# MLP of a hybrid attention block: weights loaded half a pair ahead, the up product's accumulators outside the down product's ring, rectification on ScalarE

## The chip, the cores and the metric

The kernel runs on one core of a Trainium2 chip. A core has a tensor engine (PE; its weight loads are listed as PEld), a vector engine (VectorE, DVE), a scalar engine (ScalarE, ACT), GpSimd (POOL) and a sync engine (SP) whose queue issues the DMA transfers here. Every engine takes its own instructions in the order of the program and waits on semaphores for the others. The metric is the device time of one execution in microseconds; lower is better.

## The reference

One transformer block on 1024 tokens of width 1024: a norm, an input projection, two kinds of attention (a mixture of dilated windows, and a compressed, selected and windowed one), an output projection with a residual, and an MLP with a squared rectifier. The change is in the MLP alone:

```python
h = rms_norm(h_res, norm_mlp[l])                       # 1024 tokens x 1024
h_res = h_res + jnp.square(jax.nn.relu(h @ w_up[l])) @ w_down[l]   # hidden width 4096
return rms_norm(h_res, norm_final)
```

## The kernel before, in words

The attention part fills about the first 700 us of the execution; then the MLP runs to the end. All matrices are float32. A product keeps float32's accuracy by splitting each operand into a rounded part and a residual (`hi` and `lo`) and adding three matmuls: hi with hi, lo with hi, hi with lo. `split` (line 92) makes the two parts: a copy on ScalarE writes `hi` (line 94), a subtraction on VectorE writes `lo` (line 95).

**Pairs.** The hidden width is cut into 16 pairs of 256 columns, `g` = 0 to 15. A pair has two blocks of 128 columns, f = 0 and 1. The tokens are cut into two halves of 512, h = 0 and 1.

**First matrix (up).** The pair's product is two column blocks by two token halves, with the inner width 1024 in two halves as well: a two by two block product. It is done with seven block products in place of eight, y1 to y7 (`prod`, line 1059), each 4 x 3 = 12 matmuls of 128x512 into one PSUM bank, 84 a pair. The weight combinations for them are made by `w_prep` and `w_split` from four raw blocks: RW[g, 0] to RW[g, 3], in buffers `cA`, `r3`, `r2` and `cB`; the split weights lie in `wa` to `we` (`wa` serves y1 and y5, `wb` y4 and y3, `wc` y6, `wd` y2, `we` y7). The token combinations (B11, B21, B22, T1 to T4) are made once, at the start of the MLP. The four results, of shape 128 columns x 512 tokens, are

```
c11 = y1 + y2                c12 = y1 + y6 + y5 + y3
c21 = (y1 + y6 + y7) - y4    c22 = (y1 + y6 + y7) + y5
```

so c12 and c22 are sums that live in a buffer from the first term to the last. c11 and c21 are of the first token half, c22 and c12 of the second.

**Rectification.** `c_done` (line 1069) squares the rectified result in place on VectorE (line 1071: max with 0, times itself), copies it to `uh` on ScalarE (1072), and subtracts on GpSimd for the residual `ul` (1073). The four pairs of `uh` and `ul` lie in v0, v1 (c11), v2, v3 (c21), u0, u1 (c12) and u2, u3 (c22).

**Second matrix (down).** `down` (line 1113) takes the eight tiles of 128 tokens in turn, the first half's four first. For each tile and each of two halves of 512 output columns one bank collects 2 x 3 = 6 matmuls (lines 1124 to 1126; `dn` is the split w_down of the pair, one tile for each f), and VectorE adds the bank, times the norm's factor of each token, to the residual stream `st` (line 1127). 16 banks, 96 matmuls a pair. The raw w_down blocks are loaded by `d_load` into u2 and u3, two blocks for each, and split by `d_split`. The last pair's `down` adds the final norm and the stores.

**Buffers and banks.** Each named buffer exists once, so a new tile of a name waits for the last reader of the old one. PSUM has eight banks of 128x512: rings T (2), O (2), F (1) and S (3). Before the change, y1 and y6 take T, y4 and y7 O, y2 F, and y5 and y3 take S, which is also the ring of `down`.

**What sets the order.** A scheduler orders every engine's instructions when the program is built, by the priority of the program's own order and by its estimates of when inputs and buffers are ready; the order is then fixed. It mixes the pairs: part of the up product of pair g + 1 runs between the down products of pair g.

## Time and profile before

| | us |
|---|---|
| median of 3 runs (lowest, highest) | 1413.13 (1410.70, 1417.88) |
| profiled execution, its own time | 1414.72 |
| span of that execution, first to last instruction | 1412.9 |
| mean granted tensor clock, share of full speed | 0.98 |
| PE, PEld busy | 1313.4, 1110.6 |
| DVE, ACT, POOL busy | 970.4, 650.3, 512.0 |

A row of a timeline gives the start in microseconds from the span's start, the duration, the engine, the line, the operation, output and inputs by the program's names without numbers, a count, and in brackets how long the engine had been idle before it and what it waited for. A row of a group ends with the busy time, the mean duration of one in ns, and the idle time ahead of the group by what ended it. In a row of windows each engine has its busy time and in parentheses its instructions; then come the granted clock, the DMA engines' busy share and GB/s. A few matmul records are missing from the trace, and matmuls overlap, so their starts tell more than their durations.

### The profile page before, as it was taken

Reading aid. Unit: us, or ns where it says so; the run is one execution under the profiler, and the core shown is the slowest. Engines: PE = TensorE matmul, PEld = TensorE weight load, DVE = VectorE, ACT = ScalarE, POOL = GpSimd, SP = SyncE. Lnnn points to the kernel's source line nnn. Section 1 sums busy time; section 2 is a strip of 40 time slices with the busy share of each in tenths; the row PEclk is TensorE's granted clock in tenths of the full one; section 3 lists DMA queues with packets and bytes.
Section 4 is the critical chain, followed back from the end, with each engine's and each line's share of the span. In section 5 each row is a group of like instructions: output and inputs, shape, how many; then the busy total and the mean of one; then the engine's idle time right before and its main releaser. Section 6 shows DMA issues by size and latency. Waiting matters only on the chain.

```text
span 1412.9 us, 23742 instructions
## 1 busy us (share of the span) xinstructions
PE 1313.4 (93%) x8891; PEld 1110.6 (79%) x8891; DVE 970.4 (69%) x1953; ACT 650.3 (46%) x1212; POOL 512.0 (36%) x724
## 2 busy tenths in 40 slices
PE   7999999998987999899778999999999999999996
PEld 6788989888976777677656888888888888788885
DVE  6664565773458876878587667677767667776767
ACT  7462755872557866898553222222222212222216
POOL 3445473664445665577542110011111001111115
PEclk9999999999898999999999999999999999999998
DMA  6265382985538986686311121112111111111113
GB/s 189 68 113 120 87 185 51 206 184 145 93 107 180 172 152 129 143 157 96 82 30 34 56 59 46 45 46 60 45 60 46 59 41 50 55 50 61 45 46 134
DMA packets 265747, 131.68 MB, mean 93 GB/s; under 512 B 220064, under 2 KB 240544, under 8 KB 265632
## 3 DMA queue, kind: packets, MB, share of 16 engines
q1 hardware_dynamic: 265488, 129.90, 40.0%
q8 instruction: 70, 1.15, 0.3%
q14 instruction: 45, 0.37, 0.1%
q10 hardware_dynamic: 144, 0.26, 0.0%
HBM read 68.26 MB, written 8.39 MB: 54 GB/s over the span
## 4 chain that ended last, share of the span: by engine, by line
PE 57%; DVE 16%; DMA 8%; issue 7%; POOL 6%; ACT 5%; SPq 1%; DVEq 0%; POOLq 0%; ACTq 0%
PE S L1124 8%; PE S L1125 7%; PE S L1126 7%; PE F L335 3%; PE F L336 3%; PE F L337 3%; DMA u<-in_w_down_dram 3%; PE O L1064 2%; PE O L1063 2%; PE T L1065 2%; PE T L1063 2%; PE T L1064 2%; PE O L1065 2%; PE S L418 2%; DVE c L1071 1%
## 5 line engine op out<-in xcount | busy, mean ns | idle before, releaser
L1073 POOL TENSOR_TENSOR ul<-c,uh 128x512 fp32r<-128x512 f32 x64 | 92.5, 1454 | 557.8 <-ACT uh L1072 555.9
L1127 DVE SCALAR_TENSOR_TENSOR st<-S,r,st 128x512 f32<-128x512 f32 (+1 forms) x257 | 185.8, 742 | 70.3 <-PE S L1126 69.7
L1124 PE MATMUL S<-dn,uh 128*128 128x512 f32 (+1 forms) x514 | 203.2, 396 | 9.6 <-DVE c L1110 5.9
L1126 PE MATMUL S<-dn,ul 128*128 128x512 f32 (+1 forms) x514 | 200.6, 391 | 0.8 <-POOL ul L1073 0.8
L1125 PE MATMUL S<-dn,uh 128*128 128x512 f32 (+1 forms) x514 | 200.8, 391 | 0.0
L335 PE MATMUL F<-wh,hh 128*128 128x256 f32 (+1 forms) x576 | 167.2, 292 | 6.1 <-DVE st L214 3.2
L336 PE MATMUL F<-wl,hh 128*128 128x256 f32 (+1 forms) x576 | 166.5, 289 | 2.3 <-DVE wl L95 2.3
L337 PE MATMUL F<-wh,hl 128*128 128x256 f32 (+1 forms) x576 | 165.4, 288 | 0.0
L1124 PEld LDWEIGHTS S<-dn,uh 128*128 128x128 f32 x514 | 97.2, 189 | 37.8 <-DVE c L1110 12.2
L434 ACT ACTIVATE ns<-ns,mn 128x640 f32<-128x640 f32 (+7 forms) x152 | 110.7, 747 | 35.1 <-POOL mn L433 21.7
L335 PEld LDWEIGHTS F<-wh,hh 128*128 128x128 f32 x576 | 110.7, 193 | 8.2 <-DVE st L214 3.6
L450 POOL TENSOR_TENSOR hl<-ns,hl 128x640 f16<-128x640 f32 (+5 forms) x67 | 105.5, 1575 | 30.9 <-ACT hl L448 24.9
L1126 PEld LDWEIGHTS S<-dn,ul 128*128 128x128 f32 x514 | 97.0, 189 | 22.0 <-POOL ul L1073 1.5
L336 PEld LDWEIGHTS F<-wl,hh 128*128 128x128 f32 x576 | 111.3, 193 | 3.7 <-DVE wl L95 3.1
L1125 PEld LDWEIGHTS S<-dn,uh 128*128 128x128 f32 x514 | 97.4, 190 | 19.2
L337 PEld LDWEIGHTS F<-wh,hl 128*128 128x128 f32 x576 | 111.0, 193 | 0.5
L448 ACT ACTIVATE hl<-ns 128x640 f16<-128x640 f32 (+5 forms) x115 | 91.2, 802 | 5.8 <-DMA pt<-hl 5.0
L468 PE MATMUL O<-v,pt 128*128 128x65 f16 x694 | 77.3, 195 | 15.9 <-DMA pt<-hl 13.4
L1081 ACT ACTIVATE c<-T 128x512 f32<-128x512 f32 x15 | 9.0, 599 | 172.2 <-PE S L1125 172.2
L468 PEld LDWEIGHTS <-pt 128*128 128x128 f16 x694 | 63.9, 99 | 27.6 <-DMA pt<-hl 17.4
L418 PE MATMUL S<-kb,qb 128*128 128x384 f32 (+3 forms) x192 | 72.9, 385 | 12.6 <-DVE mn L429 8.9
L433 POOL TENSOR_SCALAR mn<-mn 128x1 f32<-128x1 f32 x130 | 43.7, 336 | 96.4 <-DVE mn L429 81.2
(372 smaller groups left out, 3625.1 us busy)
## 6 DMA issues: line engine op xcount, KB each, us to landing
u<-in_w_down_dram SPq DMA_DIRECT2D x64, 256.0 KB, 2.8
wr<-in_w_in_dram SPq DMA_DIRECT2D x44, 256.0 KB, 2.9
r<-in_w_up_dram SPq DMA_DIRECT2D x32, 256.0 KB, 2.7
st<-in_x_dram SPq DMA_DIRECT2D x8, 512.0 KB, 5.9
wor<-in_w_out_dram SPq DMA_DIRECT2D x16, 256.0 KB, 3.5
cA<-in_w_up_dram SPq DMA_DIRECT2D x16, 256.0 KB, 2.8
cB<-in_w_up_dram SPq DMA_DIRECT2D x16, 256.0 KB, 2.6
ns<-in_xT_dram SPq DMA_DIRECT2D x7, 512.0 KB, 5.1
```

Source lines behind the costliest of these rows:

```text
L335: pe.matmul(ps, hh[:, k, ts], hi, start=k == 0, stop=False)
L336: pe.matmul(ps, hh[:, k, ts], lo, start=False, stop=False)
L337: pe.matmul(ps, hl[:, k, ts], hi, start=False, stop=k == KD - 1)
L418: pe.matmul(ps[:, :w], u["q"], u["k"][:, cs], start=True, stop=False)
L434: u["exp"] = act.activation(ns[:, :n * 128], ns[:, :n * 128], AF.Exp, scale=-1.0, bias=mn[:, j:j + 1])
L450: pool.tensor_sub(lo, p, hi)
L468: pe.matmul(ps, ph, v[:, 64:129], start=t == 0, stop=False)
L1073: pool.tensor_sub(lo, a, f32(hi))
L1124: pe.matmul(ps, uh[:, ts], wd[:, 0, cs], start=j == 0, stop=False)
L1125: pe.matmul(ps, uh[:, ts], wd[:, 1, cs], start=False, stop=False)
L1126: pe.matmul(ps, ul[:, ts], wd[:, 0, cs], start=False, stop=j == 1)
L1127: dve.scalar_tensor_tensor(o[:, cs], ps, r2[:, t:t + 1], o[:, cs], op0=OP.mult, op1=OP.add)
```

## The change

Five things change in the MLP, and the order of the engines follows from them.

1. `d_load`: from pair 1 on, the four w_down blocks have four buffers, v0 to v3 (those of the first token half's `uh` and `ul`), and are requested in the middle of the pair before, after its fifth down tile. All four splits stand at the head of `up`.
2. `w_load`: all four raw w_up blocks of the next pair are requested in the middle of `up`, where two of them were requested after it. For that, c12 has a buffer of its own, `x`, and c22 takes u0, after c11.
3. Banks: y2 and y7 move to T, y5 to O and y3 to F, so S is left to `down` alone.
4. `c_done`: ReLU and Square on ScalarE, both in place, then `split`: a copy on ScalarE and a subtraction on VectorE. GpSimd does none of it.
5. With the third, the second half's results (`f1`: c22, with y5 added to c12; `f2`: c12) are written into the program after the first and the second down tile (`c_rest`), where they stood at the end of `up`. The steps of `w_prep` keep their places.

```diff
     def d_load(g, q):
         j, c = q % 2, q // 2
-        t = RD[g, q] = small("u%d" % (2 + j))
+        t = RD[g, q] = small("v%d" % q if g else "u%d" % (2 + j))
...
     def c_done(g, f, h, a):
         hi, lo = U[g, f, h] = [small(x, F32R, "uh" if n == 0 else "ul") for n, x in enumerate(UT[f, h])]
-        dve.scalar_tensor_tensor(a, a, 0.0, a, op0=OP.max, op1=OP.mult)
-        act.activation(hi, a, AF.Copy)
-        pool.tensor_sub(lo, a, f32(hi))
+        act.activation(a, a, AF.Relu)
+        act.activation(a, a, AF.Square)
+        split(hi, lo, a)
 
     def up(g):
-        y = {n: bank(x, [128, 512], 2) for n, x in ((1, "T"), (4, "O"), (6, "T"), (2, "F"), (7, "O"), (5, "S"), (3, "S"))}
-        for q in range(2):
-            d_load(g, q)
+        y = {n: bank(x, [128, 512], 2) for n, x in ((1, "T"), (4, "O"), (6, "T"), (2, "T"), (7, "T"), (5, "O"), (3, "F"))}
+        for q in range(4):
+            d_split(g, q)
         prod(g, 1, y[1])
         c11 = small("u0", name="c11")
         act.activation(c11, y[1], AF.Copy)
         w_split(g, 5, "a", RW[g, 2])
-        for q in range(2):
-            d_split(g, q)
-        for q in range(2, 4):
-            d_load(g, q)
         prod(g, 4, y[4])
         prod(g, 6, y[6])
-        c12 = small("cA", name="c12")
+        c12 = small("x", name="c12")
         dve.tensor_add(c12, y[6], c11)
         w_split(g, 3, "b", RW[g, 1])
-        w_load(g + 1, 2, "r2")
-        w_load(g + 1, 1, "r3")
+        for blk, tag in enumerate(("cA", "r3", "r2", "cB")):
+            w_load(g + 1, blk, tag)
         prod(g, 2, y[2])
         dve.tensor_add(c11, y[2], c11)
         c_done(g, 0, 0, c11)
         prod(g, 7, y[7])
-        c22 = small("cB", name="c22")
+        c22 = small("u0", name="c22")
...
         c_done(g, 1, 0, c21)
-        for q in range(2, 4):
-            d_split(g, q)
         prod(g, 5, y[5])
-        dve.tensor_add(c22, y[5], c22)
-        dve.tensor_add(c12, y[5], c12)
-        c_done(g, 1, 1, c22)
         prod(g, 3, y[3])
-        dve.tensor_add(c12, y[3], c12)
-        c_done(g, 0, 1, c12)
+        return c_rest(g, y, c12, c22)
+
+    def c_rest(g, y, c12, c22):
+        def f1():
+            dve.tensor_add(c22, y[5], c22)
+            dve.tensor_add(c12, y[5], c12)
+            c_done(g, 1, 1, c22)
+
+        def f2():
+            dve.tensor_add(c12, y[3], c12)
+            c_done(g, 0, 1, c12)
+
+        return [f1, f2]
...
         else:
-            w_load(g + 1, 0, "cA")
-            w_load(g + 1, 3, "cB")
-        jobs = [] if last else w_prep(g + 1)
+            late += w_prep(g + 1)
         for i, t in enumerate(TO):
             down(g, t, last)
-            if i >= 2 and jobs:
-                jobs.pop(0)()
+            if late:
+                late.pop(0)()
+            if i == 4 and not last:
+                for q in range(4):
+                    d_load(g + 1, q)
```

The code ahead of the loop, which does pair 0, is changed in the same way.

**VectorE at the end of a middle pair's up product**, where the four results are made. Before (c with its number is one result's buffer, `dn` the split w_down):

```order
L1099 TENSOR_TENSOR c22_12882<-O_12785,c12_12843 128x512
L1071 SCALAR_TENSOR_TENSOR c11_12804<-c11_12804 128x512
L95 TENSOR_TENSOR dn_12809<-u2_12788,dn_12809 128x512
L1101 SCALAR_TENSOR_TENSOR c21_12884<-O_12782,c22_12882 128x512
L95 TENSOR_TENSOR dn_12812<-u3_12790,dn_12812 128x512
L1071 SCALAR_TENSOR_TENSOR c21_12884<-c21_12884 128x512
L1106 TENSOR_TENSOR c22_12882<-S_12786,c22_12882 128x512
L1107 TENSOR_TENSOR c12_12843<-S_12786,c12_12843 128x512
L1071 SCALAR_TENSOR_TENSOR c22_12882<-c22_12882 128x512
L1110 TENSOR_TENSOR c12_12843<-S_12787,c12_12843 128x512
```

The same place with the change (line numbers are its own from here: 1091 adds y2 to c11, 1095 and 1097 make c22 and c21, 1105 and 1106 add y5, 1110 adds y3):

```order
L95 TENSOR_TENSOR dn_12521<-v3_12458,dn_12521 128x512
L1091 TENSOR_TENSOR c11_12540<-T_12514,c11_12540 128x512
L95 TENSOR_TENSOR wd_12754<-r3_12576,wd_12754 128x512
L1040 TENSOR_TENSOR r3_12576<-r3_12576,cB_12580 128x512
L95 TENSOR_TENSOR we_12782<-cA_12574,we_12782 128x512
L95 TENSOR_TENSOR ul_12596<-c11_12540,uh_12595 128x512
L1095 TENSOR_TENSOR c22_12613<-T_12515,c12_12569 128x512
L1097 SCALAR_TENSOR_TENSOR c21_12615<-O_12512,c22_12613 128x512
L95 TENSOR_TENSOR wa_12848<-r2_12578,wa_12848 128x512
L1105 TENSOR_TENSOR c22_12613<-O_12516,c22_12613 128x512
L1106 TENSOR_TENSOR c12_12569<-O_12516,c12_12569 128x512
L1110 TENSOR_TENSOR c12_12569<-F_12517,c12_12569 128x512
```

The four splits of w_down stand together ahead of c11, the line-1071 operations are gone and residuals `ul` have come in, y5 and y3 are read from O and F, and preparations of the next pair's weights stand between.

**PE where a middle pair's down product begins.** Before, after y3 and the next pair's y2 (bank F):

```order
L1064 MATMUL F_13388<-B21l_10413,wd_13330 128x512
L1124 MATMUL S_13238<-dn_13111,uh_13167 128x512
L1125 MATMUL S_13238<-dn_13111,uh_13167 128x512
L1065 MATMUL F_13388<-B21h_10406,wd_13330 128x512
L1126 MATMUL S_13238<-dn_13111,ul_13168 128x512
L1124 MATMUL S_13238<-dn_13114,uh_13188 128x512
L1125 MATMUL S_13238<-dn_13114,uh_13188 128x512
```

With the change, after y2 and y7 of the pair and y1 of the next (bank T):

```order
L1065 MATMUL T_13429<-B11h_10405,wa_13322 128x512
L1126 MATMUL S_13259<-dn_13130,uh_13207 128x512
L1127 MATMUL S_13259<-dn_13130,uh_13207 128x512
L1126 MATMUL S_13267<-dn_13130,uh_13207 128x512
L1127 MATMUL S_13267<-dn_13130,uh_13207 128x512
L1126 MATMUL S_13283<-dn_13130,uh_13207 128x512
L1127 MATMUL S_13283<-dn_13130,uh_13207 128x512
L1128 MATMUL S_13259<-dn_13130,ul_13208 128x512
L1128 MATMUL S_13267<-dn_13130,ul_13208 128x512
L1128 MATMUL S_13283<-dn_13130,ul_13208 128x512
L1063 MATMUL T_13431<-T2h_10409,wc_13347 128x512
```

The first three banks now take their f = 0 matmuls together, nine of them; then come y6 (12 matmuls), y4 (12) and three matmuls of y5 of the next pair, the same banks' nine with f = 1, nine of y5, nine of y3, 18 of the down product, the last three of y3 and 60 of the down product. y2 and y7 of the next pair follow those directly.

**PE in the last pair.** Before, the down product follows y5 and y3 (bank S):

```order
L1065 MATMUL S_15203<-B22h_10407,wb_15261 128x512
L1124 MATMUL S_15349<-dn_15225,uh_15277 128x512
L1125 MATMUL S_15349<-dn_15225,uh_15277 128x512
L1126 MATMUL S_15349<-dn_15225,ul_15278 128x512
L1124 MATMUL S_15349<-dn_15228,uh_15298 128x512
```

With the change it follows y7:

```order
L1065 MATMUL T_15269<-T3h_10410,we_15230 128x512
L1126 MATMUL S_15398<-dn_15272,uh_15341 128x512
L1127 MATMUL S_15398<-dn_15272,uh_15341 128x512
L1126 MATMUL S_15408<-dn_15272,uh_15341 128x512
L1127 MATMUL S_15408<-dn_15272,uh_15341 128x512
```

The order of the products has turned: y5 and y3 come early, y2 and y7 last, and the down product's first operands, c11 and c21, are made from those last two.

More of the change, by code (lines that the diff above doesn't have):

```diff
@@ L1192, in build @@
         d_load(0, q)
-    w_load(1, 2, "r2")
-    w_load(1, 1, "r3")
+    for blk, tag in enumerate(("cA", "r3", "r2", "cB")):
+        w_load(1, blk, tag)
     c1 = small("u0", name="c1")
@@ L1210, in build @@
     c_done(0, 0, 0, c11)
-    c12, c22, c21 = small("cA", name="c12"), small("cB", name="c22"), small("u1", name="c21")
+    c12 = small("x", name="c12")
     dve.tensor_add(c12, y[6], c1)
+    c22, c21 = small("u0", name="c22"), small("u1", name="c21")
     dve.tensor_add(c22, y[7], c12)
@@ L1220, in build @@
         d_split(0, q)
-    dve.tensor_add(c22, y[5], c22)
-    dve.tensor_add(c12, y[5], c12)
-    c_done(0, 1, 1, c22)
-    dve.tensor_add(c12, y[3], c12)
-    c_done(0, 0, 1, c12)
+    late = c_rest(0, y, c12, c22)
     dve.tensor_mul(e2, r2, r2)
@@ L1232, in build @@
         if g:
-            up(g)
+            late = up(g)
         if last:
```

## The prediction

> **What bounds the kernel now.** I read the table of engines first, then the mean clock of the core, then a table of the MLP cut into pairs, and last the waits and the timeline at a pair's end.
>
> ```profile
> PE 1313.4 (93%) x8891; PEld 1110.6 (79%) x8891; DVE 970.4 (69%) x1953; ACT 650.3 (46%) x1212; POOL 512.0 (36%) x724
> ...
> core 0: us, PE busy (x) PEld busy (x) DVE busy (x) ACT busy (x) POOL busy (x), PEclk, DMA share, GB/s
> 799.63:841.32 41.69, 41.15 (x180) 33.61 (x180) 28.94 (x43) 9.67 (x16) 5.80 (x4) 1.00 0.17 51
> ...
> 1298.68:1340.42 41.74, 41.13 (x181) 33.65 (x181) 29.03 (x43) 9.75 (x16) 5.83 (x4) 1.00 0.17 51
> sum 540.79, PE 535.88 PEld 437.23 DVE 376.66 ACT 125.95 POOL 75.08; mean PE 41.22 PEld 33.63 DVE 28.97 ACT 9.69 POOL 5.78
> ```
>
> The two rows are the first and the last of 13 windows, each from one pair's first stalled matmul to the next pair's; the sum gives 540.79 / 13 = 41.60 us a pair. The tensor engine is busy almost throughout at full clock, so the question is how far a pair stands above pure streaming. A pair is 84 matmuls of the up products and 96 of the down products, 180. The spacing of a stream without waits is in the first three rows below, three matmuls per 0.68 us, 0.2267 us each.
>
> ```profile
> 951.68 0.39 PE L1063 MATMUL O<-T3h,we 128*128 128x512 f32 x1
> 952.36 0.39 PE L1063 MATMUL O<-T3h,we 128*128 128x512 f32 x1
> 953.04 0.39 PE L1063 MATMUL O<-T3h,we 128*128 128x512 f32 x1
> ...
> 965.28 0.39 PE L1126 MATMUL S<-dn,ul 128*128 128x512 f32 x1
> 965.35 0.68 DVE L1110 TENSOR_TENSOR c<-S,c 128x512 f32<-128x512 f32 x1
> 966.08 0.50 PE L1124 MATMUL S<-dn,uh 128*128 128x512 f32 x1 [0.41 <-DVE c L1110]
> 966.42 0.39 PE L1125 MATMUL S<-dn,uh 128*128 128x512 f32 x1
> ...
> PE S L1124 <- DVE c L1110: 5.9, 14, 0.6
> ```
>
> 180 x 0.2267 = 40.80 us, so a pair loses 0.80 us. Most of it is one place: after 965.28 the next matmul starts 0.80 us later instead of 0.227, and the one after it 0.34 later, so 0.57 + 0.11 = 0.68 us. The down product wants its third S bank, and that bank still holds y3, which line 1110 drains last in VectorE's queue. The waits view counts 14 of these, one of them in the last pair (0.64, below); the other 13 leave it idle for (5.9 - 0.64) / 13 = 0.40 us each. Why line 1110 is late:
>
> ```profile
> 955.50 6.00 SPq L1050 DMA_DIRECT2D u<-in_w_down_dram  x4
> 958.59 1.28 ACT L94 ACTIVATE dn<-u 128x512 fp32r<-128x512 f32 x2 [3.10 <-DMA u<-in_w_down_dram]
> 960.47 1.83 POOL L1073 TENSOR_TENSOR ul<-c,uh 128x512 fp32r<-128x512 f32 x1 [31.96 <-ACT uh L1072]
> 961.06 1.78 DVE L1071 SCALAR_TENSOR_TENSOR c<-c 128x512 f32<-128x512 f32 x1
> ...
> L1071 DVE SCALAR_TENSOR_TENSOR c<-c 128x512 f32<-128x512 f32 x56 | 64.5, 1151 | 0.0
> L1073 POOL TENSOR_TENSOR ul<-c,uh 128x512 fp32r<-128x512 f32 x56 | 80.9, 1453 | 501.4 <-ACT uh L1072 501.4
> L1072 ACT ACTIVATE uh<-c 128x512 fp32r<-128x512 f32 x56 | 35.2, 629 | 71.6 <-DVE c L1071 43.0 <-DVE dn L95 28.6
> L1130 ACT ACTIVATE sqj<-st 128x512 f32<-128x512 f32 x15 | 9.3, 620 | 2.2 <-DVE sso L1134 1.1 <-DVE st L1127 1.0
> L95 DVE TENSOR_TENSOR dn<-u,dn 128x512 fp32r<-128x512 f32 x56 | 37.1, 682 | 7.7 <-ACT dn L94 7.7
> L1110 DVE TENSOR_TENSOR c<-S,c 128x512 f32<-128x512 f32 x14 | 9.5, 677 | 0.0
> ```
>
> The w_down blocks are requested only when the old ones' buffers fall free, at 955.50, ScalarE waits 3.10 us for them, and the rectification then takes 1.78 us on VectorE while GpSimd runs (0.68 when it does not; 1.151 in the mean).
>
> **The change, part by part.** Removed per pair: four line-1071 operations on VectorE (4 x 1.151 = 4.6 us) and four on GpSimd (4 x 1.453 = 5.8). Added: four residual subtractions on VectorE (4 x 0.682 = 2.7) and eight activations. Square has a row in the last pair (0.620); ReLU has none. The nearest are the copies, 0.599 (line 1081, below) and 0.629, and twice a copy, 1.2, is the other bound; I take 0.63, since all three rows lie there: 8 x 0.63 = 5.0 us. No load of a function table is added: the changed order of ScalarE has one, at its start, like the old. ScalarE goes from 9.7 to 14.7 of 41 us, VectorE from 29.0 to 27.1. Neither is near the tensor engine's 40.8, which hides both as long as each chain meets its matmul.
>
> The Trainium skill, ScalarE: Activation LUTs, section Rules for kernel authors, speaks against this: ReLU, max and multiply belong on VectorE, which it puts at up to about three times ScalarE's speed (in bf16). An estimate with that factor, 3 x 0.682 = 2.0 us an activation, would bring the first half 3 us past its matmul in every pair, some 45 us in all. The rows above disagree for this shape and type: 0.620 and 0.629 on ScalarE against 0.682 on VectorE. I go by the rows.
>
> **The wait that goes.** No down product takes a bank from y5 or y3 any more: they lie in O and F, and the S ring serves only the down product. So the 14 stalls end. At the quoted pair 0.41 us of idle time cost 0.68 of spacing, so the mean of 0.40 costs 0.67: 13 x 0.67 = 8.7, and the one pair's end that the view does not name adds at most as much again: 9.2 us in all. The other 0.13 us per pair is loose spacing after a stall; I count half of it as saved, 1.0 us.
>
> **The wait that comes.** In the changed order y2 follows the last down matmul directly, and it wants the T bank of y1, which ScalarE copies to c11. That copy needs buffer u0, free once the last down tile has read it. Before:
>
> ```profile
> 954.40 0.39 PE L1125 MATMUL S<-dn,uh 128*128 128x512 f32 x1
> 954.89 0.60 ACT L1081 ACTIVATE c<-T 128x512 f32<-128x512 f32 x1 [11.63 <-PE S L1125]
> 955.52 0.69 DVE L1090 TENSOR_TENSOR c<-T,c 128x512 f32<-128x512 f32 x1 [2.88 <-ACT c L1081]
> ```
>
> From the matmul that frees u0 to the copy's consumer: 955.52 - 954.40 = 1.12 us. After that matmul four more follow, so y2 would start 5 x 0.2267 = 1.13 us after it. It comes out even; with the weight load not taken ahead (the 0.11 above) 0.13 us a pair, 15 pairs: 2.0 us lost. Bounds: 0 and 0.3 us a pair (4.5).
>
> **The cover of the longer chains.** Times from the start of y2. VectorE first has the last evacuation and the four w_down residuals (five operations, 0.60 apart), so c11 is added at 3.7, ReLU 4.4, square 5.0, ScalarE's copy into we 5.9 (it waits for y7, which ends at 5.44), uh ready at 7.2, residual 7.9, c22 8.5, c21 9.1. The down product is due after y2, y7 and the next y1, 36 matmuls or 8.16 us: 1.0 us to spare (0.4 if a ReLU takes 1.2). Its second half (c21) is ready at about 12.6 and due after 9 down, y6, y4 and a quarter of y5 at 16.3: 3.7 to spare. y6 wants y7's bank at 10.2, drained at 8.5. Second-half tiles are due 16 us later still. The w_down loads go when the first-half tiles have been read, 48 matmuls or 10.9 us before y2; two issues take 0.80 us and a landing 2.8 (median), so four are there with 6 us to spare. In the steady part nothing else is late.
>
> ```profile
> 997.08 0.80 SPq L1050 DMA_DIRECT2D u<-in_w_down_dram  x2
> ...
> u<-in_w_down_dram SPq DMA_DIRECT2D x56, 256.0 KB, 2.8
> ```
>
> **The last pair** has no next y1. Before, y5 and y3 stood ahead of the last down product, and it still stalled:
>
> ```profile
> 1377.09 0.39 PE L1124 MATMUL S<-dn,uh 128*128 128x512 f32 x1
> 1378.20 0.50 PE L1126 MATMUL S<-dn,ul 128*128 128x512 f32 x1 [0.49 <-POOL ul L1073]
> 1379.41 0.50 PE L1124 MATMUL S<-dn,uh 128*128 128x512 f32 x1 [0.71 <-ACT uh L1072]
> 1381.92 0.79 PE L1124 MATMUL S<-dn,uh 128*128 128x512 f32 x1 [0.64 <-DVE c L1110]
> 1383.37 0.63 PE L1124 MATMUL S<-dn,uh 128*128 128x512 f32 x1
> ...
> 1380.00:1384.00 4.00, 3.09 (x8) 2.07 (x8) 4.00 (x6) 1.50 (x3) 1.34 (x2) 0.67 0.00 0
> 1384.00:1388.00 4.00, 4.00 (x17) 3.21 (x17) 3.00 (x5) 2.54 (x7) 4.00 (x4) 0.91 0.00 0
> ```
>
> From 1377.09, where the down product starts, the next seven matmuls of the order take 4.83 us, 1.6 us of work: 3.2 lost; then the granted clock falls to 0.67 and 0.91 (of four microseconds each, (0.33 + 0.09) x 4 = 1.7 us). Together 4.9. Now y7 ends at 5.44 with nothing behind it. By the sums above without the we copy, uh is ready at 6.4 (1.1 lost), nine matmuls run to 8.6, c21's half is ready at 10.9 (2.4 lost), and the three banks then end together and are drained behind a residual, 14.0 against 13.0 (1.1 lost): 4.6, and the clock's loss on top, 1 to 2.5. So 6.4, 1.5 worse (0 to 3).
>
> **The first pair.** Before, the down product of pair 0 starts amid stalls:
>
> ```profile
> 749.11 0.50 PE L1124 MATMUL S<-dn,uh 128*128 128x512 f32 x1 [0.64 <-DVE c L1213]
> 751.75 0.50 PE L1124 MATMUL S<-dn,uh 128*128 128x512 f32 x1 [1.23 <-DVE c L1214]
> 753.61 0.80 PE L1124 MATMUL S<-dn,uh 128*128 128x512 f32 x1 [0.90 <-ACT uh L1072]
> 756.97 0.39 PE L1126 MATMUL S<-dn,ul 128*128 128x512 f32 x1
> ```
>
> The changed order puts y1, y4 and part of y5 of pair 1 there, as cover; but their weights' preparation (five more VectorE operations ahead of c21, 3 us) comes earlier too. Walking VectorE's and ScalarE's new order with the durations above, the residual of wa (pair 1, y5) is ready at 756.9, where the matmul comes at 755.4, and that of wc (y6) at 759.9 against 758.1: two stalls of 1.5 and 1.8 us. By 760.2 us 36 matmuls are then done since the first row quoted, and 35 were before. I take 0, bounds -2 (loss) and +3.
>
> **Sum.** 9.2 + 1.0 - 2.0 - 1.5 + 0 = 6.7 us. The profiled execution took 1414.72 (span 1412.9); the median shown is 1413.13, and a saving of matmul waits is the same number of microseconds in either: 1413.13 - 6.7 = 1406.4. Bounds: 9.2 - 4.5 - 3 - 2 gives 0, so 1413; 10.2 + 0 + 0 + 3 gives 13, so 1400. Likeliest one's own range: 1402 to 1411.
>
> **Rivals.**
> *The stall only moves*: y2 is held by the c11 copy for as long as the old stall, because ScalarE, strictly in order, is still at a weight split when u0 falls free. For: the same u0 dependence, 0.01 us of margin. Against: ScalarE is idle 11.63 us before that copy. 15 x 0.7 replaces 9.2, and the last pair costs its 1.5: 1414 to 1416. 14%.
> *Slower: the first half's chain misses its matmul.* Place: c11 to uh, now an add, three activations and a residual behind four w_down residuals in VectorE's queue. It decides from 1.0 us of slip; at 2 us each of 15 pairs loses 1 us more, and a slip of that kind costs 15 - 6.7 = 8.3: 1421. For: every link adds a semaphore hop. Against: the hops in the rows are 0.03 to 0.10 us. 8%.
> *The start gains too and the end loses nothing*: pair 1's products cover all of pair 0's stalls (3 us), y2 never waits: 1400 to 1403. For: the idle times in pair 0's three rows sum to 2.8 us, and a slower spacing follows them. Against: VectorE is already full there. 14%.
>
> **How the numbers follow.** The forecast has 64%. About 0.5% (7.1 us, 1406.1) is what a measurement of this kernel can tell from no change. The forecast lies on that edge: 31 of its 64 parts are faster, 33 within. With the gaining rival faster is 45%; with the moved stall within is 47%; slower 8%. The range, 1400 to 1413, leaves out the slow rival, the moved stall's far part and a little below.
>
> **What would show it.** Right: no wait of a down matmul for a VectorE sum in pairs 1 to 14; windows of a pair at 40.9 to 41.1 us; a wait of y2 for the line-1081 copy of at most 0.3 us; GpSimd without work in the MLP until the end; the last pair's gaps before the second and third group of nine, 4 to 5 us, with a fall of the clock. Wrong: pairs still at 41.6, or waits of the down product for uh or ul in every pair.

## The result, and the profile after

The changed kernel takes 1406.62 us in the median of 8 runs (1402.91 to 1409.77), the kernel before beside it 1416.85 (1410.70 to 1421.88): a ratio of 0.9926, with a 95% interval of 0.9908 to 0.9945. That is faster by 0.74%, 10.2 us by the medians. The forecast was 1406.4, made from a saving of 6.7 us and a start of 1413.13; that start was the median of three runs and lay 3.7 us under the later one. So the saving was undersized by 3.5 us, and the time came out right because two errors met, which is luck.

The profiled execution of the changed kernel has a span of 1403.6 us (before: 1412.9). First its table of engines, then windows of one pair each, from one pair's first y2 matmul to the next pair's (columns as before; the first and the last of twelve, and their sum):

```profile
PE 1317.0 (94%) x8891; PEld 1118.6 (80%) x8891; DVE 970.1 (69%) x1953; ACT 718.9 (51%) x1340; POOL 420.4 (30%) x660
```

```profile
826.52:867.40 40.88, 40.88 (x181) 33.73 (x181) 28.61 (x43) 14.00 (x25) 0.00 (x0) 1.00 0.17 52
...
1276.27:1317.16 40.89, 40.89 (x182) 33.75 (x181) 28.62 (x43) 14.01 (x25) 0.00 (x0) 1.00 0.17 52
sum 490.64, PE 490.64 PEld 404.87 DVE 343.45 ACT 168.01 POOL 0.00; mean PE 40.89 PEld 33.74 DVE 28.62 ACT 14.00 POOL 0.00
```

A pair takes 490.64 / 12 = 40.89 us where it took 41.60; pure streaming is 40.80. PE is busy for the whole of each window and GpSimd does nothing. The waits view names what is left of the 0.09 us: the weight load of y2, once a pair, for the copy of y1 to c11.

```profile
PEld T L1063 <- ACT c L1081: 3.1, 15, 0.3
```

The wait of the down product for the sum on VectorE (5.9 us, 14 times, before) is no longer there. The last pair, in the timeline of PE:

```profile
1363.35 0.39 PE L1065 MATMUL T<-T3h,we 128*128 128x512 f32 x1
1364.37 0.50 PE L1126 MATMUL S<-dn,uh 128*128 128x512 f32 x1 [0.64 <-ACT uh L94]
...
1365.87 0.84 PE L1128 MATMUL S<-dn,ul 128*128 128x512 f32 x3
1368.98 0.80 PE L1126 MATMUL S<-dn,uh 128*128 128x512 f32 x1 [2.27 <-ACT uh L94]
1369.57 0.63 PE L1127 MATMUL S<-dn,uh 128*128 128x512 f32 x1
1370.00 0.63 PE L1126 MATMUL S<-dn,uh 128*128 128x512 f32 x1
```

y7 ends, the down product waits 0.64 us for the first `uh`, runs nine matmuls, and waits 2.27 us for the second. After that pause the matmuls start 0.43 us apart instead of 0.23: the clock has fallen.

To compare kernels I cut the MLP of each into three stretches and count what each **loses** against streaming, that is, its time less 0.2267 us for every matmul that the order has in it (the last twelve, half as wide, count whole, and four small transposes at the start are left out, alike in all kernels). The first stretch begins at the second residual matmul of y4 in pair 0 (735.11 us before, 735.94 after) and ends at the first y2 of pair 1; the second ends at the first y2 of pair 15; the third at the last matmul. Before: (757.43 - 735.11) - 48 x 0.2267 = 11.4, (1335.34 - 757.43) - 2504 x 0.2267 = 10.3, (1403.51 - 1335.34) - 281 x 0.2267 = 4.5. After: (785.57 - 735.94) - 188 x 0.2267 = 7.0, (1358.05 - 785.57) - 2520 x 0.2267 = 1.2, (1392.83 - 1358.05) - 125 x 0.2267 = 6.4. The sum falls from 26.2 to 14.7 us. Against that stand 0.8 us of an attention part that came out longer in this one execution and 1.4 us more behind the last matmul (9.4 before, 10.8 after): 11.5 - 0.8 - 1.4 = 9.3, the difference of the spans.

All kernels of this study by the same count, and their times against the kernel before, run beside them. The experiments ran on three chips, and a ratio compares a kernel with the runs of the kernel before beside it, so it is not the quotient of two medians of the table:

| kernel | start | 14 pairs | last pair | sum lost, us | median, us | ratio (95%) |
|---|---|---|---|---|---|---|
| before | 11.4 | 10.3 | 4.5 | 26.2 | | 1 |
| changed | 7.0 | 1.2 | 6.4 | 14.7 | 1406.62 | 0.9926 (0.9908 to 0.9945) |
| before, new banks alone | 12.1 | 50.6 | 0.8 | 63.4 | 1456.36 | 1.0297 (1.0275 to 1.0318) |
| before, new rectification alone | 10.5 | 13.6 | 2.9 | 27.0 | 1417.94 | 1.0010 (0.9988 to 1.0032) |
| before, all early loads alone | 6.0 | -0.1 | 6.7 | 12.6 | 1403.09 | 0.9915 (0.9890 to 0.9940) |
| before, early w_down alone | 11.6 | -0.1 | 0.7 | 12.2 | 1403.83 | 0.9897 (0.9866 to 0.9927) |
| changed, old rectification | 5.9 | 2.2 | 5.6 | 13.7 | 1402.44 | 0.9915 (0.9894 to 0.9936) |
| changed, old banks | 6.1 | -0.1 | 2.5 | 8.5 | 1395.92 | 0.9858 (0.9830 to 0.9885) |
| changed, old banks and old rectification | 6.0 | -0.1 | 6.7 | 12.6 | 1398.51 | 0.9877 (0.9851 to 0.9904) |

### The profile page after: what moved, and what is told of

It is laid out like the page before. It is cut to its first block, busy times and chain, and to the rows that moved or that the text cites. A ratio compares the mean times of both kernels' runs of the same rounds, so it can differ in the third digit from the quotient of the medians.

```text
span 1403.6 us, 23694 instructions
## 1 busy us (share of the span) xinstructions
PE 1317.0 (94%) x8891; PEld 1118.6 (80%) x8891; DVE 970.1 (69%) x1953; ACT 718.9 (51%) x1340; POOL 420.4 (30%) x660
## 4 chain that ended last, share of the span: by engine, by line
PE 65%; DVE 12%; POOL 6%; issue 6%; DMA 6%; ACT 5%; SPq 1%; POOLq 0%; DVEq 0%; ACTq 0%
PE S L1126 8%; PE S L1127 8%; PE S L1128 8%; PE T L1063 4%; PE T L1065 4%; PE T L1064 4%; PE F L335 3%; PE F L336 3%; PE F L337 3%; DMA pt<-hl 2%; PE O L1065 2%; PE O L1064 2%; PE O L1063 2%; PE S L418 2%; POOL hl L450 1%
## 5 line engine op out<-in xcount | busy, mean ns | idle before, releaser
L1129 DVE SCALAR_TENSOR_TENSOR st<-S,r,st 128x512 f32<-128x512 f32 (+1 forms) x257 | 189.3, 747 | 92.9 <-PE S L1128 92.7
L1133 POOL TENSOR_TENSOR y<-st,gfin 128x512 f32<-128x512 f32 x7 | 9.5, 1354 | 631.3 <-DVE st L1129 628.4
L1128 PE MATMUL S<-dn,ul 128*128 128x512 f32 (+1 forms) x514 | 194.7, 390 | 0.0
L469 PE MATMUL O<-v,pt 128*128 128x64 f16 x694 | 76.9, 194 | 0.0
```

What stands on the lines that cost most here:

```text
L1128: pe.matmul(ps, ul[:, ts], wd[:, 0, cs], start=False, stop=j == 1)
L1129: dve.scalar_tensor_tensor(o[:, cs], ps, r2[:, t:t + 1], o[:, cs], op0=OP.mult, op1=OP.add)
```

## The experiments

My theory was that the third S bank, held by y3, is the stall, and that moving the banks takes it away. The rivals were that the late w_down loads are the cause, and that the gain at the start comes from GpSimd leaving the rectification.

**One part of the change alone.** First the banks, in the kernel before:

```diff
-        y = {... (2, "F"), (7, "O"), (5, "S"), (3, "S")}
+        y = {... (2, "T"), (7, "T"), (5, "O"), (3, "F")}
```

> The kernel before with the new banks alone (y2 and y7 in T, y5 in O, y3 in F); loads, sums and rectification as before. Theory (the pair-end stall is the third S bank, held by y3): pairs of 40.9 to 41.1 us instead of 41.60, no wait of a down product for the sum in pairs 1 to 13, start of the MLP as before, so 7 to 9 us faster, 1406 to 1408 beside 1415. Rival (the late w_down loads and VectorE's long queue are the cause; the bank only shows them): the wait comes back at uh or at another bank, pairs stay at 41.4 to 41.6, under 3 us faster.

It is 3% slower. A pair takes 44.4 us. One pair's end, from the timelines of PE, and of ScalarE (the last three rows):

```profile
931.59 0.50 PE L1124 MATMUL S<-dn,uh 128*128 128x512 f32 x1 [0.79 <-ACT uh L1072]
934.18 0.50 PE L1124 MATMUL S<-dn,uh 128*128 128x512 f32 x1 [0.23 <-ACT uh L1072]
938.09 0.50 PE L1124 MATMUL S<-dn,uh 128*128 128x512 f32 x1 [1.53 <-DVE st L1127]
...
919.12 0.60 ACT L1081 ACTIVATE c<-T 128x512 f32<-128x512 f32 x1 [9.34 <-PE S L1125]
922.77 1.28 ACT L94 ACTIVATE dn<-u 128x512 fp32r<-128x512 f32 x2 [3.06 <-DMA u<-in_w_down_dram]
926.81 0.63 ACT L94 ACTIVATE dn<-u 128x512 fp32r<-128x512 f32 x1 [2.76 <-DMA u<-in_w_down_dram]
```

The wait for the sum has gone, as the theory said, but the down product now waits for `uh` and for its own evacuation. y2 and y7 need y1's T bank, which ScalarE copies only after the last down tile (919.12); so they run behind it, and c11 is late. And the w_down blocks come in two late lots, 3.06 and 2.76 us of waiting; VectorE has its last w_down residual at 928.38 and takes the first rectification at 930.19:

```profile
928.38 0.69 DVE L95 TENSOR_TENSOR dn<-u,dn 128x512 fp32r<-128x512 f32 x1 [0.21 <-ACT dn L94]
928.99 0.68 DVE L1095 TENSOR_TENSOR c<-T,c 128x512 f32<-128x512 f32 x1
...
930.19 0.68 DVE L1071 SCALAR_TENSOR_TENSOR c<-c 128x512 f32<-128x512 f32 x1
```

The last matmul of y2 starts at 926.34, but its sum (line 1095) stands behind the w_down residuals until 928.99: with the banks moved, the same lateness shows at `uh`. This run doesn't tell whether y5 and y3 alone out of S, with y2 and y7 left in their places, would have ended the stall; no run did that.

The rectification alone, in the kernel before:

```diff
-        dve.scalar_tensor_tensor(a, a, 0.0, a, op0=OP.max, op1=OP.mult)
-        act.activation(hi, a, AF.Copy)
-        pool.tensor_sub(lo, a, f32(hi))
+        act.activation(a, a, AF.Relu)
+        act.activation(a, a, AF.Square)
+        split(hi, lo, a)
```

> The kernel before with the rectification alone changed (ReLU and square on ScalarE, residual on VectorE). Theory (bank; and the gain at the start of the MLP comes from GpSimd leaving it): the bank stays, VectorE reaches the sum of y3 a little earlier, pairs 41.2 to 41.6; the stretch from the MLP's start to the first pair's end gains 2 to 4.5 us; together 3 to 9 us faster. Rival (the start's gain comes from pair 1's products put there as cover, not from GpSimd): the start gains under 1 us, at most 5 us faster in all.

No difference (1.0010). A stall of the same size stays in the pair's first down tiles, but its releaser is now an evacuation:

```profile
1092.27 0.39 PE L1126 MATMUL S<-dn,ul 128*128 128x512 f32 x1
1093.09 0.50 PE L1124 MATMUL S<-dn,uh 128*128 128x512 f32 x1 [0.43 <-DVE st L1127]
```

Here too the second bank is left for want of w_down; the three banks end within four matmuls of each other, are drained in one piece, and the fourth waits. And the start loses 10.5 us, 0.9 less than before: GpSimd's leaving is not what shortens it.

The loads alone (both kinds, with c12 in `x`, c22 in `u0` and four splits at the head of `up`; banks, rectification and the place of the sums are old):

```diff
-        t = RD[g, q] = small("u%d" % (2 + j))
+        t = RD[g, q] = small("v%d" % q if g else "u%d" % (2 + j))
...
+            if i == 4 and not last:
+                for q in range(4):
+                    d_load(g + 1, q)
...
-        w_load(g + 1, 2, "r2")
-        w_load(g + 1, 1, "r3")
+        for blk, tag in enumerate(("cA", "r3", "r2", "cB")):
+            w_load(g + 1, blk, tag)
```

> The kernel before with the early loads alone (w_down and the pair's weights half a pair ahead, all four w_down splits at the head of a pair); old banks, old rectification, sums where they were. Theory (bank): the stall shrinks, since ScalarE no longer waits 3.10 us for w_down, but the bank is still in the ring: pairs 41.0 to 41.5, 1 to 7 us faster. Rival (the late loads are the whole cause): pairs 40.9, 8 to 9 us faster, as much as the banks alone.

The rival holds: the loads alone give the whole steady gain, with the old banks. The first of its windows, all of the same length:

```profile
794.32:835.12 40.80, 40.80 (x181) 33.78 (x180) 30.64 (x43) 9.61 (x17) 5.81 (x4) 1.00 0.17 53
```

Its pairs take 40.80 us, streaming to the last hundredth, which the changed kernel does not reach. The start also loses only 6.0 us. Its last pair is worse than before (6.7), in the timelines of PE and VectorE:

```profile
1367.15 0.50 PE L1120 MATMUL S<-dn,ul 128*128 128x512 f32 x1 [0.62 <-POOL ul L1073]
1370.05 0.70 PE L1118 MATMUL S<-dn,uh 128*128 128x512 f32 x1 [2.40 <-ACT uh L1072]
...
1367.13 0.69 DVE L1095 TENSOR_TENSOR c<-O,c 128x512 f32<-128x512 f32 x1 [2.11 <-POOL ul L1073]
```

c22 took c11's buffer u0, since its own, `cB`, is now filled early with weights. So the sum of c22 (line 1095) waits 2.11 us until GpSimd has read c11 for `ul`, and c21 behind it.

**Which of the loads.** Only the w_down part of the last kernel, with `w_load` and the buffers of c12 and c22 as before:

> The kernel before with only w_down loaded half a pair ahead and split at the head of a pair; the up products' weights are loaded as before, and banks, sums and rectification are the old ones. Theory (the stall came from VectorE reaching the sum of y3 late, because ScalarE waited 3.10 us for w_down): the wait of the down product for y3's sum is gone or under 0.1 us, pairs of 40.8 to 41.0 us, 9 to 11 us faster than before. Rival (the up weights' earlier loads count, since they put the next pair's first products ahead of the down product as cover): pairs of 41.2 to 41.6, at most 5 us faster.

The steady loss is gone, and the last pair's nearly so. How early w_down does it is seen in pair 5, the pair whose end the prediction quotes, in two views. First the order of PE's instructions at the start of its down product, with buffer numbers (`S_12332`, `S_12340` and `S_12348` are the first, second and third bank; `S_12348` is y3's). Before:

```order
L1126 MATMUL S_12332<-dn_12205,ul_12262 128x512
L1124 MATMUL S_12332<-dn_12208,uh_12282 128x512
L1125 MATMUL S_12332<-dn_12208,uh_12282 128x512
L1124 MATMUL S_12340<-dn_12205,uh_12261 128x512
L1126 MATMUL S_12332<-dn_12208,ul_12283 128x512
L1124 MATMUL S_12348<-dn_12205,uh_12261 128x512
L1125 MATMUL S_12348<-dn_12205,uh_12261 128x512
```

With early w_down:

```order
L1119 MATMUL S_12332<-dn_12195,uh_12286 128x512
L1118 MATMUL S_12340<-dn_12192,uh_12265 128x512
L1119 MATMUL S_12340<-dn_12192,uh_12265 128x512
L1120 MATMUL S_12340<-dn_12192,ul_12266 128x512
L1118 MATMUL S_12340<-dn_12195,uh_12286 128x512
L1119 MATMUL S_12340<-dn_12195,uh_12286 128x512
L1120 MATMUL S_12332<-dn_12195,ul_12287 128x512
L1120 MATMUL S_12340<-dn_12195,ul_12287 128x512
L1118 MATMUL S_12348<-dn_12192,uh_12265 128x512
```

Before, the second bank gets one matmul and is left: it collects output columns 512 to 1023, and the residuals of w_down for these come only with the second lot of loads. So the third bank is taken after seven matmuls of the down product; with w_down there, after twelve. Second, the timelines: VectorE before, behind the sum of y3; then, of the new kernel, VectorE in pair 5, and PE there.

```profile
965.35 0.68 DVE L1110 TENSOR_TENSOR c<-S,c 128x512 f32<-128x512 f32 x1
965.95 1.28 DVE L95 TENSOR_TENSOR dn<-u,dn 128x512 fp32r<-128x512 f32 x2
```

```profile
956.49 1.89 DVE L95 TENSOR_TENSOR dn<-v,dn 128x512 fp32r<-128x512 f32 x3
...
962.01 0.68 DVE L1071 SCALAR_TENSOR_TENSOR c<-c 128x512 f32<-128x512 f32 x1
962.61 0.69 DVE L1104 TENSOR_TENSOR c<-S,c 128x512 f32<-128x512 f32 x1
...
964.24 0.39 PE L1118 MATMUL S<-dn,uh 128*128 128x512 f32 x1
...
966.96 0.39 PE L1118 MATMUL S<-dn,uh 128*128 128x512 f32 x1
```

The last w_down residuals ended at 967.2 before, behind y3's sum; they now end at 958.4. y3's sum (line 1104 in this kernel) starts 0.9 us after y3's last matmul (961.29 + 0.39) in place of about 4 us, and the third bank is due at 966.96, 3.7 us after the sum's end; before, it was due at 965.51 and the sum ended at 966.03. In the next pair VectorE is as late as before, and the later place of the third bank alone is enough, with 0.5 us to spare (the sum ends at 1007.30, and the twelfth matmul after 1005.04 is due at 1007.76):

```profile
1006.62 0.68 DVE L1104 TENSOR_TENSOR c<-S,c 128x512 f32<-128x512 f32 x1
```

In pair 5 the earlier sum would have been enough even at the bank's old place, where it would be due at some 965.8; in the next pair only the later place is. The two kinds alternate: in seven pairs y3's sum starts 4.1 us after y3's end, no earlier than before (3.7 to 4.2), in six 0.9 us. With all loads it starts even later, 10.3 us after y3's end (957.69 in the pair below), and nothing waits, since the third bank is taken 63 matmuls after y3, where it was 19 before and is 24 with early w_down. The sum on VectorE and the third bank's first matmul in the kernel with all loads:

```profile
967.97 0.68 DVE L1104 TENSOR_TENSOR c<-S,c 128x512 f32<-128x512 f32 x1
971.80 0.39 PE L1118 MATMUL S<-dn,uh 128*128 128x512 f32 x1
```

So what the pairs without a stall have in common is the order, in which the third bank comes later, and not an earlier sum. The early loads and the splits' place at the head of `up` were moved together; neither was tried without the other.

But the start is as before (11.6): the up products' early weights are what shortens it. Beside early w_down alone, the kernel with all loads gains 5.6 us at the start and loses 6.0 in the last pair. Here the down product of pair 0 still stalls, in the timeline of PE, where the kernel with all loads runs y1 of pair 1:

```profile
752.64 0.50 PE L1118 MATMUL S<-dn,uh 128*128 128x512 f32 x1 [0.64 <-DVE c L1207]
...
755.28 0.51 PE L1118 MATMUL S<-dn,uh 128*128 128x512 f32 x1 [1.21 <-DVE c L1208]
```

```profile
753.46 0.40 PE L1063 MATMUL T<-B11h,wa 128*128 128x512 f32 x1
```

**One part of the change undone.** The changed kernel with the old rectification (the diff of the rectification, reversed):

> The changed kernel with the old rectification put back (one operation on VectorE, copy on ScalarE, residual on GpSimd). Theory (banks and loads make the pairs, GpSimd's absence makes the start): pairs stay 40.9 to 41.0, the start gives back 2 to 4.5 us, so 2 to 5 us slower than the changed kernel, 1408.5 to 1411.5 where that has 1406.6. Rival (cover at the start, not GpSimd): no difference to the changed kernel beyond 1 us. Second rival (the rectification is what the first half's chain needs): waits of the down product for uh in every pair, pairs over 41.2, no better than the kernel before.

The start loses 5.9 us, even a little less than in the changed kernel (7.0); the pairs are 40.96. The time can't be told from the changed kernel's. The first theory of its start, GpSimd, has fallen here for the second time.

The changed kernel with the old banks (the diff of the banks, reversed):

> The changed kernel with the old banks put back (y2 in F, y7 in O, y5 and y3 in S); early loads, late sums and the new rectification stay. New theory, after the banks alone made pairs of 44.4 us and the loads alone pairs without a stall: the early loads carry the whole gain and the banks none, so pairs of 40.8 to 41.0 us, no slower than the changed kernel by more than 2 us (1404 to 1408.5). Old theory (the third S bank, held by y3, is the stall, and with the sums now behind the first down tile it is held even longer): a wait of the down product for y3's sum or an evacuation in each of 14 pairs, pairs of 41.3 to 41.9 us, 6 to 14 us slower than the changed kernel.

This has the lowest median of all, 1.4% under the kernel before. Its interval lies wholly below the changed kernel's; it overlaps those of early w_down alone and of two kernels below. One window of its pairs, and its last pair in the timeline of PE:

```profile
788.22:829.02 40.80, 40.80 (x181) 33.80 (x180) 27.77 (x43) 13.68 (x24) 0.00 (x0) 1.00 0.17 53
```

```profile
1359.87 0.39 PE L1128 MATMUL S<-dn,ul 128*128 128x512 f32 x1
1362.07 0.50 PE L1126 MATMUL S<-dn,uh 128*128 128x512 f32 x1 [1.81 <-DVE c L1106]
1362.41 0.40 PE L1127 MATMUL S<-dn,uh 128*128 128x512 f32 x1
```

No steady stall, though y5 and y3 hold S banks and their sums stand behind the first down tile in the program. Once, in the last pair, the S bank does stall (1.81 us); the clock stays up. The new banks cost 1.3 us in the pairs (y2 waiting for c11's copy), 3.9 in the last pair (y2 and y7 can't run before the last down tile, and y5 and y3 no longer stand as cover ahead of the down product) and 0.9 at the start. By this count the move that I took for the gain is a loss of some 6 us.

Both undone:

> Early loads and late sums, with the old banks and the old rectification: the kernel with the old banks, and its rectification undone. Theory (the rectification matters only where nothing covers its chain): pairs stay at 40.8, the last pair loses 4 to 6 us where the new rectification lost 2.5, since its chain through VectorE and GpSimd is longer there: 2 to 4 us slower than with the new one (1398 to 1400 where that has 1396). Rival (the place of the sums made the short last pair, not the rectification): within 1 us of it.

The profile says 4.2 us more in the last pair, as in the kernel with the loads alone, to which its three losses are equal. The traces of these two show the same instructions in the same order on every engine, so with the old banks and the old rectification the late sums do nothing; with the new banks no run tells. They are one program measured twice: the medians were 1403.09 and 1398.51 us, the ratios 0.9915 and 0.9877, while the losses agree within 0.1 us. Beside that, the 2.6 us between the medians with the new and the old rectification show nothing, and the intervals overlap; the 4.2 us rest on the profiles. With the old banks the new rectification is thus worth something in one place: VectorE, not GpSimd, reads c11 last, and u0 is free sooner.

**The slack of the first half's chain.** Three more ReLUs in place for each block of pairs 1 to 15, and then one more:

```diff
         act.activation(a, a, AF.Relu)
+        if g:
+            for _ in range(3):
+                act.activation(a, a, AF.Relu)
```

> The changed kernel with each ReLU of pairs 1 to 15 done four times over (three more activations in place, which change nothing in the result), so each c chain is 3 x 0.63 = 1.9 us longer. In the changed kernel's trace uh of the first half is ready 1.3 us and ul 1.0 us (two matmuls later than uh) ahead of the down product. Theory (the chain's slack is about one us, beyond it every us counts): the down product waits 0.6 to 0.7 us for uh and some 0.3 for ul in each pair, 14 x 0.9 = 12 us slower than the changed kernel, between 8 and 16, and the last pair 2 to 4 us more. Rival (ScalarE, 14 of 41 us busy, has room, and the cover is larger than the walk says): under 3 us.

> The changed kernel with each ReLU of pairs 1 to 15 done twice. With three more the wait for uh was 1.24 us in each pair, so three had lengthened the chain by about 1.24 + 1.34 = 2.6 us, 0.86 each. Theory (a threshold at 1.0 to 1.3 us of slack): one more is hidden, pairs of 40.9 to 41.0 us without a wait for uh. Rival (no threshold, every added us counts in part): a third of the cost of three, pairs of 41.7.

With three more, 1440.14 us (ratio 1.0166, 1.0139 to 1.0193), pairs of 518.46 / 12 = 43.20 us, 2.3 longer; the start loses 7.6 us, the last pair 11.4. PE at one pair's end and later in it:

```profile
1048.76 0.39 PE L1065 MATMUL T<-B11h,wa 128*128 128x512 f32 x1
1050.39 0.50 PE L1129 MATMUL S<-dn,uh 128*128 128x512 f32 x1 [1.24 <-ACT uh L94]
...
1109.21 0.50 PE L1129 MATMUL S<-dn,uh 128*128 128x512 f32 x1 [0.39 <-DVE st L1132]
```

With one more, 1406.94 us in its one run; pairs of 40.96 us, 0.07 over the changed kernel; the last pair, where nothing covers the chain, loses 8.7 us in place of 6.4:

```profile
826.23:867.19 40.96, 40.96 (x181) 33.71 (x180) 28.61 (x43) 16.11 (x29) 0.00 (x0) 1.00 0.17 52
```

So there is a threshold, and the slack lies between one ReLU (0.63 us) and three. That three cost 2.3 us a pair and not 0.9 has two reasons in the trace: the longer chain made the copy into `wa` go ahead of `uh` on ScalarE (at 1092.36 and 1092.90 us in one pair), so the chain grew by 2.8 us (`uh` is ready 9.7 us after the start of y2, 6.9 in the changed kernel), half of it slack and half lateness; and a late evacuation stalls the product once more.

**The last pair.** Two tries to shorten it. The first gives c11, c22 and c21 of the last pair other buffers, so that its products run among the down products of pair 14:

```diff
-        c11 = small("u0", name="c11")
+        c11 = small("cA" if g == NP - 1 else "u0", name="c11")
-        c22 = small("u0", name="c22")
+        c22 = small("cB" if g == NP - 1 else "u0", name="c22")
-        c21 = small("u1", name="c21")
+        c21 = small("r2" if g == NP - 1 else "u1", name="c21")
```

> The changed kernel with other buffers for c11, c22 and c21 in the last pair only (those of weights that are not loaded any more), so that the copy of y1 does not wait for u0 and the products of the last pair run among the down products of pair 14. Theory (the last pair's stalls come from y2 being held until the last down tile, with nothing behind it): down product of the last pair without the waits for uh and without the half clock, the last pair's loss of 6.4 us falls to 1 to 2, the rest as in the changed kernel: 4.5 to 5.5 us faster than it, about 1401.5. Rival (the chain just waits elsewhere, earlier in the same stretch, or the tail grows): under 1.5 us.

> The same buffers in the last pair, with the old rectification (VectorE, ScalarE, GpSimd). Theory: the last pair's loss of 5.6 us, as the changed kernel with the old rectification had it, falls to 1 to 2: 1397.5 to 1399, and 2 to 4 us under the same buffers with the new rectification, since the first pair keeps its smaller stalls and the longer chain no longer matters at the end. Rival (the rectification makes no difference anywhere): the two within 1 us of each other.

No gain: 1405.21 us (0.9908, 0.9879 to 0.9936) and 1405.17 (0.9916, 0.9889 to 0.9944). The last pair loses 5.6 and 5.0 us. Of the first, ScalarE and PE:

```profile
1365.84 0.63 ACT L94 ACTIVATE uh<-c 128x512 fp32r<-128x512 f32 x1 [2.37 <-PE S L1127]
1366.38 1.13 ACT L94 ACTIVATE dn<-v 128x512 fp32r<-128x512 f32 x2
...
1366.26 0.39 PE L1128 MATMUL S<-dn,ul 128*128 128x512 f32 x1
1369.65 0.79 PE L1126 MATMUL S<-dn,uh 128*128 128x512 f32 x1 [3.00 <-ACT uh L94]
```

The sums are ready long before, but `uh` and the split w_down (`dn`) exist once, and both can be written only when pair 14's last down tiles have read them. Between two pairs' down products there must be some microseconds of other matmuls; I had moved that cover away.

The second takes the kernel with the old banks and moves y5 to T and y3 to F in the last pair alone:

```diff
-        y = {... (5, "S"), (3, "S")}
+        y = {... (5, "T" if g == NP - 1 else "S"), (3, "F" if g == NP - 1 else "S")}
```

> The kernel with the old banks (early loads, late sums, new rectification), and in the last pair alone y5 in T and y3 in F, so that no sum holds an S bank there. Theory (what is left of the bank's stall: 1.81 us of wait for y5's sum, 1.97 of spacing, once): the wait goes, 1.5 to 2 us faster than without, about 1394. Rival (y5 now waits for the c11 copy and y3 for c11's sum, and gives it back): within 0.5 us of it.

1399.45 us (0.9880, 0.9857 to 0.9902): not faster, and its last pair loses 3.5 us instead of 2.5. The wait for the sum is gone, and the first nine matmuls run; then one for `uh` stands in its place:

```profile
1358.02 0.84 PE L1128 MATMUL S<-dn,ul 128*128 128x512 f32 x3
1360.19 0.50 PE L1126 MATMUL S<-dn,uh 128*128 128x512 f32 x1 [1.34 <-ACT uh L94]
```

It is the same picture as the whole study: the bank shows a lateness that lies in the chain behind it.

## Why the prediction was right, and where it was not

- **"The wait that goes" (9.2 us, and 1.0 of spacing): right in size, wrong in cause.** I had written both halves of the cause, that the bank holds y3 and that w_down is late, and put the gain down to the banks. The runs put it down to w_down: early w_down alone takes the steady loss from 10.3 us to nothing, the banks alone raise it to 50.6. Of w_down's lateness I had seen the way through VectorE's queue, and not the way through the order, in which the third bank was taken before the second could be filled; that is the one which all pairs without a stall share. The 50.6 come with y2 and y7 held by T, so they say that these banks as a set do not cure it, not that no move of banks could.
- **"The wait that comes" (0.13 us a pair): right in place**, and 0.09 in size, 1.2 us over 14 pairs for 2.0 over 15. It exists only because of the new banks.
- **The first pair (0, bounds -2 and +3): mis-sized.** It gained 11.4 - 7.0 = 4.4 us. Of the two stalls that I walked out for wa and wc (1.5 and 1.8 us), one came, of 0.61 us idle:

```profile
756.31 0.39 PE L1128 MATMUL S<-dn,ul 128*128 128x512 f32 x1
757.30 0.50 PE L1063 MATMUL T<-T2h,wc 128*128 128x512 f32 x1 [0.61 <-ACT wc L94]
```

  I had bounded the gain by the idle times of pair 0's rows, and left out the slower spacing that follows them. Part of that spacing is the clock: before, the granted clock was 0.57 in the mean of four microseconds there, a loss of 0.43 x 4 = 1.7 us; with the change it was 1.00. The rows before and after:

```profile
753.00:757.00 4.00, 3.39 (x9) 2.70 (x10) 4.00 (x6) 1.82 (x3) 1.48 (x2) 0.57 0.03 10
...
753.00:757.00 4.00, 3.69 (x17) 2.73 (x15) 4.00 (x8) 2.57 (x5) 0.00 (x0) 1.00 0.28 74
```

  This term is where the saving was undersized.
- **The last pair (1.5 us worse, 0 to 3): 6.4 - 4.5 = 1.9 worse by the count**, with the two gaps and the fall of the clock where I had put them (0.64 for 1.1, 2.27 for 2.4, 0.29 for 1.1). The 1.4 us more behind the last matmul were not foreseen; that stretch varies between 9.4 and 10.8 us over these kernels, and no run tells why.
- **The rectification at no cost: right.** GpSimd has no work in the windows, ScalarE 14.0 us a pair (14.7 forecast), VectorE 28.6 (27.1 forecast). The Trainium skill's rule (ScalarE: Activation LUTs, Rules for kernel authors), whose factor is for bf16 and which spoke against the move, decided nothing here: ReLU and square take 0.63 us each, and alone the move gives 1.0010.
- **The slack:** 1.0 us forecast for `uh`, 1.4 in the trace (ready 6.9 us after the start of y2, needed at 8.25); for c21 3.7 forecast, 4.1 found. This is why the rival of the missed matmul did not come about. It does when the chain grows by 2.8 us.
- **The rivals.** That the stall only moves is right for the banks by themselves, and for the last pair. That the start gains is right for the start and wrong for the end.

A kernel that does the loads and keeps the old banks, with the new rectification, beats both: 1395.92 us.

## What to carry to other kernels

A wait names the resource that was still held, not why its holder was late: before moving the resource, follow the holder's queue back to the first wait on it (here ScalarE's 3.10 us for w_down), and try that cure alone. Then look in the order for when the resource is asked for: here the stall ended because the third bank came later, while its holder was often as late as before. When a change has several parts, cost each part with the others absent: here one part made the gain, one took nearly half as much back, and one was neutral by itself. And a buffer that exists once needs cover between its last reader and its next; products moved ahead to fill one gap are missing as cover in the next.

## What the runs showed of the hardware

The clock falls after long pauses of the tensor engine. After single pauses of 2.27, 2.40 and 3.00 us in the last pair (rows above) the matmuls started 0.43 us apart; after pauses of 1.81 and 1.34 us they went on at 0.23. Near 1.9 us either happened: a pause of 1.91 us in the changed kernel with the old rectification was followed by starts 0.43 us apart, one of 1.90 us at the start of the MLP before was not. Shorter pauses close together do it too: in pair 0 before, pauses of 0.64, 1.23 and 0.90 us within some five microseconds (the prediction's rows of the first pair) were followed by starts 0.43 us apart, at the granted clock of 0.57 shown above. The windows of the changed kernel's last pair show the granted clock:

```profile
1362.00:1366.00 4.00, 3.37 (x15) 2.48 (x14) 1.84 (x4) 1.89 (x3) 0.00 (x0) 1.00 0.00 0
1366.00:1370.00 4.00, 1.73 (x6) 1.08 (x5) 3.23 (x5) 3.37 (x7) 0.00 (x0) 0.87 0.00 0
1370.00:1374.00 4.00, 3.71 (x12) 2.66 (x11) 2.32 (x4) 2.48 (x6) 0.74 (x1) 0.70 0.00 0
```

So a pause can cost more than itself: after the 2.27 us another (0.13 + 0.30) x 4 = 1.7 us went with the clock. The Trainium skill (TensorE: Matmul & The Clock Gate, HAM oscillation) gives gaps over about 3.4 us as the rule; here 2.27 were enough, and the measurement decides.

The attention part, the same code in all kernels, ended up to 9 us apart from one profiled execution to the next (the first stretch begins between 731.1 and 740.3 us). A difference of a few microseconds between two single spans says nothing here; the losses counted from a fixed matmul do.
